# A hybrid encoder block on one core: a fourth place for raw weights, gelu stores on ACT's queue, and two evacuations with higher priority

## The chip, the cores and the metric

The kernel runs on one core of a Trainium2 chip. A core has TensorE (PE, with PEld its weight loads), VectorE (DVE), ScalarE (ACT), GpSimd (POOL) and SyncE (SP), an on-chip memory of 128 partitions, and a smaller accumulator memory in banks of 128x512 f32, into which PE writes. The metric is the device time of one execution in microseconds (us), the median of several runs.

## The reference

One layer for 512 positions of width 1024, everything in f32:

```python
h = _rms(x, norm_mix_g); z = h @ w_in
u_ssm, c_q, c_kv, k_rope = z[:, :512], z[:, 512:1280], z[:, 1280:1536], z[:, 1536:]
# S5 mixer: 32 groups of 16 channels, 64 complex states each, over positions
bu = einsum('gph,bsgh->bsgp', b_bar, u)
states = associative_scan(combine, (a_bar, bu))       # s <- a_bar * s + bu
y = gelu(einsum('ghp,bsgp->bsgh', c, states).real + d_skip * u)
y_ssm = y * sigmoid(y @ w_glu + b_glu)
# latent attention: 8 heads, rotary part of 32, block-causal mask in chunks of 64
q = _rms(c_q, q_norm_g) @ w_q_up;  kv = _rms(c_kv, kv_norm_g) @ w_kv_up
y_mla = softmax(mask(q k^T / sqrt(96))) v
x = x + concat(_rms(y_ssm), _rms(y_mla)) @ w_out
# cross-attention of 4 heads into 256 memory tokens
x = x + xattn(_rms(x), _rms(mem), w_q, w_k, w_v) @ w_o
# experts: best of 4 groups, then the best 2 of its 8 gated experts (hidden 256)
x = x + sum_e gate_e * (silu(h w_gate_e) * (h w_up_e)) @ w_down_e
out = _rms(x, norm_final_g)
```

## The kernel before

The whole program is one stream of instructions that a scheduler sorts for each engine when the program is built; the code gives it a priority, by the place in the program and by `tc.high_priority(n)`, which `hp_(HPW)` uses with n = 150 to put an instruction that many places ahead. Within an engine the order is then fixed: an instruction whose data is not there holds everything behind it. Each engine that issues DMAs has its own queue of such instructions, mixed with its other work; nearly all loads and stores of this kernel are issued on SP.

Weights come through a list. `next_w` takes the next weight, asks for the loads up to `LOOK` ahead (`load_w`, L167, tile `raw`, up to 512 KB), and splits the raw f32 weight into a high part `hi` (ACT, L204) and a rest `lo` (DVE, L214), of which three each are kept. A `raw` place is free when its `lo` is made. A product is three matmuls (L266 hi*hi, L267 hi*lo, L268 lo*hi).

The stages, in the order of the program: the norm of x; the S5 input `pz` (four column blocks; each is evacuated to `zq` by DVE with the row scale, L752, and stored to `zd`); the key and value latent `pkv`; the query latent `pcq` in six blocks of 24 matmuls, evacuated in `cq` (ACT and DVE) and squared into `sq_q` (ACT, L870 and L873), which DVE adds up to `sqa` for the query norm; the norm of the memory tokens (`mem`, `mT`, transposes `pT_norm_mem_g`) with `q_norm` in its middle (column sum `pc_q`, then the rotary tables `crq` and `srq` scaled by it); the query up-projection `pq` in two halves of four position blocks (pq00 to pq03, pq10 to pq13), three weights each; the memory values `pxv`; the latent's keys and values `pv`, `pkn`; attention; the glu, output, cross-attention; and from about 460 us the experts. The accumulators of `pcq`, `pq` and `pxv` share four banks, so pq03 begins where the last `pcq` block has been read.

Between these stages the S5 mixer runs in pieces for four chunk groups q = 0 to 3, each put beside a step of the main stream (`S5_PLAN`): `s5kt` (matmuls, evacuated to `s5k`, stored to `kd` and loaded back as a Toeplitz tile `s_T` by eight loads, L677), `s5vT` (transposes, evacuated to `s5VT`), `s5u` (loaded from `zd`), `s5e` (input matmuls, L696), then on DVE `s5a`, `s5b`, `s5ee`, a scan `s5s` and `s5x` (L707 to L722), `s5y` (output matmuls from `s_T`, `s5u`, `s5G`, `s5x`, L730 and L731), and gelu on ACT into `s5yz` (L735), which eight DMAs of 32 KB store to `gd` (L739), read again only for the glu.

Of the kernel before, what the change touches and what calls it, by code (L numbers as in the profile page):

```python
# [10 lines left out]
F32 = mybir.dt.float32  # L11
# [4 lines left out]
AF = mybir.ActivationFunctionType  # L16
OP = mybir.AluOpType
# [4 lines left out]
NT = 4  # L22
# [77 lines left out]
HPW = 150  # L100
# [4 lines left out]
def build(tc, I, out, dbg=None, stop=None):  # L105
    nc = tc.nc
# [16 lines left out]
    C = es.enter_context(tc.tile_pool(name="const", bufs=1))  # L123
# [1 line left out]
    U = es.enter_context(tc.tile_pool(name="u", bufs=4))  # L125
    B = es.enter_context(tc.tile_pool(name="b", bufs=4, space=PS))
    wes = es.enter_context(ExitStack())
    LOOK = 3
    M = wes.enter_context(tc.tile_pool(name="misc", bufs=2))
    W = wes.enter_context(tc.tile_pool(name="w", bufs=2))  # L130
    raw_es = wes.enter_context(ExitStack())
    WR = raw_es.enter_context(tc.tile_pool(name="raw", bufs=LOOK))
    ses = es.enter_context(ExitStack())
# [6 lines left out]
    def bank(name):  # L140
        return B.tile([128, 512], F32, name=name, tag="mm")

    def bankt(name):
        return B.tile([128, 512], F32, name=name, tag="tr", bufs=2)
# [44 lines left out]
    def next_w(name):  # L189
        i = nxt[0]  # L190
        nxt[0] += 1
        while nxt[1] < min(len(wlist), i + LOOK):
            load_w(nxt[1])
# [45 lines left out]
    for i in range(8):  # L239
# [4 lines left out]
        n, k = divmod(i, 4)  # L244
# [48 lines left out]
    load_w(0, 1)  # L293
    for i in range(1, LOOK):
        load_w(i)
    nxt[1] = LOOK

# [7 lines left out]
    ps = bankt("ps_gx")  # L305
# [3 lines left out]
    def hp_(n):  # L309
        return tc.high_priority(n) if n else nullcontext()  # L310

    def gain(name, k):
        return G[:, gcol[name] + k:gcol[name] + k + 1]
# [57 lines left out]
    def hv(k, c0=0, c1=S):  # L371
        t = hT[k // 2]
        return t[:, k % 2, 0, c0:c1], t[:, k % 2, 1, c0:c1]
# [12 lines left out]
    rx, rx2 = x_st[:, 1], x_st[:, 2]  # L386
    w0 = next_w("ssm")
    rx, rx2 = x_st[:, 1], x_st[:, 2]
# [13 lines left out]
    for t in range(NT):  # L402
        sq = M.tile([128, 2, 512], F32, name=f"xsq{t}", tag="krT", bufs=1)
# [4 lines left out]
    r = 0  # L408
# [4 lines left out]
    ps = bankt("ps_g")  # L413
# [7 lines left out]
    RX = M.tile([128, S], F32, name="RX", tag="krT", bufs=1)  # L421
# [303 lines left out]
    def s5_e(q, b):  # L725
        uu, x2 = b["uu"], b["x2"]
        ps = BS.tile([128, 512], F32, name=f"s5y{q}", tag="s")
        for g in range(8):
            o = ps[:, 64 * g:64 * g + 64]
            nc.tensor.matmul(o, b["T"][:, g], uu[:, g], start=True, stop=False)  # L730
            nc.tensor.matmul(o, b["G"][:, g, 0:8].rearrange("p k h -> p (k h)"), x2[:, g // 2, g % 2],  # L731
                             start=False, stop=True)

        z = M.tile([128, 512], F32, name=f"s5yz{q}", tag="sq")
        nc.scalar.activation(z, ps, AF.Gelu_apprx_tanh)  # L735
        gv = gd[128 * q:128 * q + 128].rearrange("(g h) (j c) -> h j g c", h=16, j=8)
        zz = z.rearrange("p (g c) -> p g c", g=8)
        for j in range(8):
            nc.sync.dma_start(gv[:, 7 - j], zz[16 * j:16 * j + 16])  # L739

    p5 = s5_params()

# [1 line left out]
    for m in range(4):  # L744
        w = next_w("ssm") if m else w0
        ps = bank(f"pz{m}")
        for k in range(8):
            mm3(ps, (w[0][:, k], w[1][:, k]), hv(k), k == 0, k == 7)
        if m == 0 and CX:
            rx_row()  # L750
        z = M.tile([128, 8, 64], F32, name="zq", tag="zq")
        nc.vector.tensor_tensor(z, ps.rearrange("p (c j) -> p j c", j=8), RX.rearrange("p (c j) -> p j c", j=8), OP.mult)  # L752
        nc.sync.dma_start(zd[128 * m:128 * m + 128], z.rearrange("p j c -> p (j c)"))
    sb = [{} for _ in range(4)]

# [22 lines left out]
    nc.vector.tensor_tensor(ang, rpf[:, :, None].to_broadcast([128, NT, 16]),  # L778
                            ivf[:, None, :].to_broadcast([128, NT, 16]), OP.mult)
    sincos(sin, cos, ang, [128, NT, 16], M, "rope")  # L780
    crx, srx = C.tile([128, NT, 16], F32, name="crx"), C.tile([128, NT, 16], F32, name="srx")
    rxb = rx[:, :, None].to_broadcast([128, NT, 16])
    nc.vector.tensor_tensor(crx, cos, rxb, OP.mult)
    nc.vector.tensor_tensor(srx, sin, rxb, OP.mult)
# [78 lines left out]
    for m in range(6):  # L863
        w = next_w("cq")
        ps = bank(f"pcq{m}")
        for k in range(8):
            mm3(ps, (w[0][:, k], w[1][:, k]), hv(k), k == 0, k == 7)
        split(cq[m // 2][:, m % 2, 0], cq[m // 2][:, m % 2, 1], ps, gain("mla_q_norm_g", m))
        if m == 0:
            nc.scalar.activation(sqa, ps, AF.Square)  # L870
        else:
            sq = M.tile([128, S], F32, name=f"sq_q{m}", tag="sq")
            nc.scalar.activation(sq, ps, AF.Square)  # L873
            nc.vector.tensor_tensor(sqa, sqa, sq, OP.add)
        step()
    rq = C.tile([128, NT], F32, name="rq")
    crq, srq = C.tile([128, NT, 16], F32, name="crq"), C.tile([128, NT, 16], F32, name="srq")

    def q_norm():
        colsum_rstd(rq, sqa, 768, "q", True)  # L880
# [79 lines left out]
    for i in range(8):  # L960
        n, c = divmod(i, 4)
# [80 lines left out]
    for hp in range(4):  # L1042
# [16 lines left out]
        else:  # L1059
            sq = M.tile([128, S], F32, name=f"sq_m{hp}", tag="sq")  # L1060
# [20 lines left out]
    for m in range(4):  # L1081
        w = next_w("glu")
        ps = bank(f"pgl{m}")
# [14 lines left out]
        else:  # L1098
            sq = M.tile([128, S], F32, name=f"sq_s{m}", tag="sq")
# [38 lines left out]
    for n in range(2):  # L1138
# [5 lines left out]
        for t in range(NT):  # L1144
            sq = M.tile([128, S], F32, name=f"xsq2{n}{t}", tag="sq")
            square_sum(st2[:, n, t:t + 1], X[t][:, n * 512:n * 512 + 512], sq)
        for k in range(4 * n, 4 * n + 4):
            ps = bankt(f"ph2{k}")
# [421 lines left out]
    for q in OQ:  # L1570
# [5 lines left out]
        else:  # L1576
            g, c = int(q[0]), int(q[1])
# [3 lines left out]
    for c in range(2):  # L1581
        ps = bankt(f"pXt0{c}")
# [70 lines left out]
    ps = bankt("ptab0")  # L1653
# [3 lines left out]
    if T1:  # L1657
        ohb1 = places_of(1)
        ps = bankt("ptab1a")
# [29 lines left out]
    ps = bankt("ptab0w")  # L1689
# [293 lines left out]
```

## Time and profile before

| | |
|---|---|
| median of 3 runs | 716.57 us (715.13 to 717.44) |
| the profiled execution | 717.67 us |
| its span in the trace | 715.9 us |
| PE busy | 666.9 us (93%) |
| DVE busy | 406.1 us (57%) |
| ACT busy | 251.8 us (35%) |
| POOL busy | 113.7 us (16%) |
| DMA moved | 165.83 MB, mean 232 GB/s |
| mean granted TensorE clock | 0.984 |

A row of a timeline gives the start, the duration, the engine, the line of the code, the operation, the output and the inputs with their shapes, and in brackets how long the engine had stood idle and for whom. "SPq" is SP's queue of DMA issues. The profiled execution is 1.1 us over the median, and the span is 1.8 us shorter than that execution's time.

### The profile page before, as it was taken

What the parts mean: (1) busy time and instruction counts of PE and PEld (TensorE: products, weight loads), DVE (VectorE), ACT (ScalarE), POOL (GpSimd) and SP (SyncE); (2) the same over time, 40 slices, a digit from 0 to 9 for tenths busy, and PEclk for the clock granted to TensorE, in tenths of its full rate; (3) what the DMA queues carried; (4) which work ended last, traced back from release to release, by engine and by line L of the source; (5) the groups of instructions that cost most, each with busy time, mean ns of one, the idle gap of its engine ahead of it and who ended that gap; (6) DMA issues with size and microseconds to landing.
All of it is one profiled execution on the core that took longest, in us unless ns stands there. A gap on an engine that the chain in (4) does not pass through costs nothing.

```text
span 715.9 us, 10163 instructions
## 1 busy us (share of the span) xinstructions
PE 666.9 (93%) x3644; PEld 469.7 (66%) x3644; DVE 406.1 (57%) x952; ACT 251.8 (35%) x518; POOL 113.7 (16%) x165
## 2 busy tenths in 40 slices
PE   5989999788999999999999999989999999999793
PEld 4788878676778888888887788734344454454342
DVE  4899988747577887565366642653443512221137
ACT  5734364325666767244344522221000000000023
POOL 6300022002400000102000001212242233233100
PEclk9999999989999999999999999999999999999988
DMA  7763233335452434323328797799999999999993
GB/s 217 199 197 99 66 79 95 79 124 125 112 191 67 147 120 118 95 83 89 91 87 314 274 334 276 240 395 410 405 412 406 411 412 404 410 411 409 381 356 128
DMA packets 102012, 165.83 MB, mean 232 GB/s; under 512 B 32762, under 2 KB 64606, under 8 KB 98120
## 3 DMA queue, kind: packets, MB, share of 16 engines
q1 hardware_dynamic: 95512, 157.58, 62.0%
q0 software_dynamic: 6432, 7.58, 3.1%
q8 instruction: 30, 0.49, 0.3%
q14 instruction: 22, 0.18, 0.1%
q10 hardware_dynamic: 16, 0.00, 0.0%
HBM read 154.59 MB, written 25.69 MB: 252 GB/s over the span
## 4 chain that ended last, share of the span: by engine, by line
PE 59%; DMA 28%; DVE 5%; ACT 4%; issue 1%; SPq 1%; POOL 1%; ACTq 0%; DVEq 0%
DMA gu<-moe_w_up 18%; DMA dn<-moe_w_down 6%; PE pG L1789 3%; PE po L1039 2%; PE pxq L268 2%; PE pxq L267 2%; PE pxq L266 2%; PE pxo L266 2%; DMA raw<-w_in 2%; PE pxo L267 2%; PE pD L1846 1%; PE pxo L268 1%; PE pcq L266 1%; PE pPT L1028 1%; PE pcq L267 1%
## 5 line engine op out<-in xcount | busy, mean ns | idle before, releaser
L1789 PE MATMUL pG<-gu,XT 128*64 128x512 f32 x512 | 120.3, 607 | 6.6 <-DMA gu<-moe_w_up 3.0
L214 DVE TENSOR_TENSOR lo<-raw,hi 128x1024 fp32r<-128x1024 f32 (+3 forms) x64 | 75.5, 1183 | 62.0 <-ACT hi L204 61.5
L204 ACT ACTIVATE hi<-raw 128x1024 fp32r<-128x1024 f32 (+3 forms) x64 | 63.9, 1002 | 107.9 <-issue 26.0
L1789 PEld LDWEIGHTS pG<-gu,XT 128*64 128x64 f32 x512 | 54.5, 139 | 58.7 <-issue 52.0
L1812 DVE SCALAR_TENSOR_TENSOR a<-pG,RS,sl 128x256 f32<-128x256 f32 x16 | 10.7, 671 | 113.2 <-ACT sl L1806 106.8
L1846 PE MATMUL pD<-dn,aT 128*64 128x512 f32 x256 | 71.1, 600 | 0.5 <-ACT aT L1832 0.5
L1806 ACT ACTIVATE sl<-pG,RS 128x256 f32<-128x256 f32 x16 | 7.6, 473 | 123.5 <-PE pG L1789 123.5
L1846 PEld LDWEIGHTS pD<-dn,aT 128*64 128x64 f32 x256 | 22.4, 137 | 35.7 <-issue 34.4
L1855 DVE SCALAR_TENSOR_TENSOR YY<-pD,GT,YY 128x512 f32<-128x512 f32 x26 | 19.5, 750 | 25.2 <-PE pD L1846 25.1
L1808 POOL TENSOR_SCALAR YY<-XG,F 128x1024 f32<-128x1024 f32 x13 | 14.5, 1116 | 114.8 <-issue 50.7
L1832 ACT ACTIVATE aT<-pA 128x256 f32<-128x256 f32 x16 | 6.1, 384 | 68.0 <-PE pA L1830 36.4
L1772 PEld LDWEIGHTS pX<-ident,XG 128*128 128x128 f32 x120 | 14.6, 194 | 16.9 <-issue 12.9
L267 PE MATMUL pxq<-gT,hi 128*128 128x512 f32 x64 | 25.6, 400 | 0.0
L266 PE MATMUL pxq<-gT,hi 128*128 128x512 f32 x64 | 25.5, 399 | 0.0
L268 PE MATMUL pxq<-gT,lo 128*128 128x512 f32 x64 | 25.4, 396 | 0.0
L1417 DVE TENSOR_TENSOR XT<-pX,gmo 128x512 f32<-128x512 f32 x30 | 19.3, 683 | 7.4 <-PE pX L1772 7.4
L1772 PE MATMUL pX<-ident,XG 128*128 128x128 f32 x120 | 17.6, 288 | 3.8 <-DMA XG<-hd,IX 3.8
L1388 POOL TENSOR_TENSOR st_moe<-st_moe 128x1 f32<-128x1 f32 x4 | 0.8, 190 | 118.6 <-issue 104.4
L266 PE MATMUL pcq<-hT,hi 128*128 128x512 f32 x48 | 19.2, 401 | 0.0
L268 PE MATMUL pcq<-hT,lo 128*128 128x512 f32 x48 | 19.1, 398 | 0.0
L267 PE MATMUL pxv<-lo,mT 128*128 128x512 f32 x32 | 13.9, 435 | 5.5 <-DVE lo L214 5.5
L267 PE MATMUL pcq<-hT,hi 128*128 128x512 f32 x48 | 18.9, 395 | 0.0
(614 smaller groups left out, 1670.6 us busy)
## 6 DMA issues: line engine op xcount, KB each, us to landing
gu<-moe_w_gate SPq DMA_DIRECT2D x64, 512.0 KB
gu<-moe_w_up SPq DMA_DIRECT2D x64, 512.0 KB
dn<-moe_w_down SPq DMA_DIRECT2D x30, 1024.0 KB
raw<-w_in SPq DMA_DIRECT2D x9, 512.0 KB
raw<-xattn_w_v SPq DMA_DIRECT2D x8, 512.0 KB
raw<-xattn_w_k SPq DMA_DIRECT2D x8, 512.0 KB
raw<-w_out SPq DMA_DIRECT2D x8, 512.0 KB
raw<-xattn_w_q SPq DMA_DIRECT2D x8, 512.0 KB
```

Source lines behind the costliest of these rows:

```text
L204: anchor["act"] = nc.scalar.activation(hi, r, AF.Copy)
L214: anchor["dve"] = nc.vector.tensor_tensor(lo, r, hi.bitcast(F32), OP.subtract)
L266: i = nc.tensor.matmul(o, lh, rh, start=start, stop=False)
L267: nc.tensor.matmul(o, lh, rl, start=False, stop=False)
L268: anchor["pe"] = nc.tensor.matmul(o, ll, rh, start=False, stop=stop)
L1039: nc.tensor.matmul(po[64 * s:64 * s + 64, b * 128:b * 128 + 128], V[:, k, 64 * h:64 * h + 64], PTs[s][:, k * 128:k * 128 + 128], start=k = ...
L1417: return v.tensor_tensor(xt, ps.rearrange("p (k t) -> p k t", k=4), gmo[:, 4 * c:4 * c + 4, None].to_broadcast([128, 4, 128]), OP.mult)
L1772: i = nc.tensor.transpose(ps[:, k * 128:k * 128 + 128], xg[:, 4 * c + k], ident)
L1789: i = nc.tensor.matmul(pg[64 * s:64 * s + 64], xt[c][:, kk, 64 * s:64 * s + 64], ew[2 * n + s, c][:, :, kk], start=k == 0, stop=k == 7)
L1808: nc.gpsimd.tensor_scalar(result(n), XG[n % 2], F1[:, n:n + 1], 1.0, OP.mult, OP.mult)
L1846: i = nc.tensor.matmul(pd[64 * s:64 * s + 64], at_[:, f, 64 * s:64 * s + 64], ew[2 * n + s, 2][:, f, c * 512:c * 512 + 512], start=f == 0, ...
L1855: yield v.scalar_tensor_tensor(o, pd, GT[:, n:n + 1], o, OP.mult, OP.add)
```

## The change

Four edits. `LOOK` goes from 3 to 4, so the raw weights have four places and are asked for one weight earlier; the memory for it comes from the rotary tables of the key (`crx`, `srx`) and of the query (`crq`, `srq`), which now share a place each. The eight gelu stores of each chunk group are issued by ACT and no longer by SP. The evacuation `zq` and the squares of the query blocks 1 to 5 are issued under the priority of 150.

```diff
@@ -125,7 +125,7 @@
     U = es.enter_context(tc.tile_pool(name="u", bufs=4))
     B = es.enter_context(tc.tile_pool(name="b", bufs=4, space=PS))
     wes = es.enter_context(ExitStack())
-    LOOK = 3
+    LOOK = 4
     M = wes.enter_context(tc.tile_pool(name="misc", bufs=2))
     W = wes.enter_context(tc.tile_pool(name="w", bufs=2))
     raw_es = wes.enter_context(ExitStack())
@@ -736,7 +736,7 @@
         gv = gd[128 * q:128 * q + 128].rearrange("(g h) (j c) -> h j g c", h=16, j=8)
         zz = z.rearrange("p (g c) -> p g c", g=8)
         for j in range(8):
-            nc.sync.dma_start(gv[:, 7 - j], zz[16 * j:16 * j + 16])
+            nc.scalar.dma_start(gv[:, 7 - j], zz[16 * j:16 * j + 16])
 
     p5 = s5_params()
 
@@ -749,7 +749,9 @@
         if m == 0 and CX:
             rx_row()
         z = M.tile([128, 8, 64], F32, name="zq", tag="zq")
-        nc.vector.tensor_tensor(z, ps.rearrange("p (c j) -> p j c", j=8), RX.rearrange("p (c j) -> p j c", j=8), OP.mult)
+        with hp_(HPW):
+            nc.vector.tensor_tensor(z, ps.rearrange("p (c j) -> p j c", j=8), RX.rearrange("p (c j) -> p j c", j=8),
+                                    OP.mult)
         nc.sync.dma_start(zd[128 * m:128 * m + 128], z.rearrange("p j c -> p (j c)"))
     sb = [{} for _ in range(4)]
 
@@ -778,7 +780,7 @@
     nc.vector.tensor_tensor(ang, rpf[:, :, None].to_broadcast([128, NT, 16]),
                             ivf[:, None, :].to_broadcast([128, NT, 16]), OP.mult)
     sincos(sin, cos, ang, [128, NT, 16], M, "rope")
-    crx, srx = C.tile([128, NT, 16], F32, name="crx"), C.tile([128, NT, 16], F32, name="srx")
+    crx, srx = (C.tile([128, NT, 16], F32, name=n + "rx", tag=n + "r") for n in "cs")
     rxb = rx[:, :, None].to_broadcast([128, NT, 16])
     nc.vector.tensor_tensor(crx, cos, rxb, OP.mult)
     nc.vector.tensor_tensor(srx, sin, rxb, OP.mult)
@@ -870,11 +872,12 @@
             nc.scalar.activation(sqa, ps, AF.Square)
         else:
             sq = M.tile([128, S], F32, name=f"sq_q{m}", tag="sq")
-            nc.scalar.activation(sq, ps, AF.Square)
+            with hp_(HPW):
+                nc.scalar.activation(sq, ps, AF.Square)
             nc.vector.tensor_tensor(sqa, sqa, sq, OP.add)
         step()
     rq = C.tile([128, NT], F32, name="rq")
-    crq, srq = C.tile([128, NT, 16], F32, name="crq"), C.tile([128, NT, 16], F32, name="srq")
+    crq, srq = (C.tile([128, NT, 16], F32, name=n + "rq", tag=n + "r") for n in "cs")
 
     def q_norm():
         colsum_rstd(rq, sqa, 768, "q", True)
```

The lines behind move by two (from L753) and by three (from L874).

What it moves, at three places. First SP's queue around the store of chunk group 1. Before (raw is a weight's load, gd the gelu store, kd, s5u and s_T belong to the next chunk group):

```order
L167 DMA raw_1548<-mla_w_q_up 128x2x384
L167 DMA raw_1613<-xattn_w_v 128x2x512
L167 DMA raw_1643<-xattn_w_v 128x2x512
L739 DMA gd<-s5yz_1349 16x8x64 x8
L673 DMA kd_220<-s5k_1398 4x32x256
L686 DMA s5u_1611<-zd 128x8x64
L167 DMA raw_1758<-xattn_w_v 128x2x512
L677 DMA s_T_379<-kd_220 16x1024
L677 DMA s_T_379<-kd_220 16x8x112
```

After:

```order
L677 DMA s_T_382<-kd_221 16x8x16
L167 DMA raw_1426<-mla_w_q_up 128x2x384
L167 DMA raw_1550<-xattn_w_v 128x2x512
L167 DMA raw_1615<-xattn_w_v 128x2x512
L686 DMA s5u_1613<-zd 128x8x64
L673 DMA kd_222<-s5k_1400 4x32x256
L167 DMA raw_1645<-xattn_w_v 128x2x512
L677 DMA s_T_381<-kd_222 16x1024
L677 DMA s_T_381<-kd_222 16x8x112
```

The eight stores are gone from this queue, and kd and s5u of the next chunk group stand one value weight earlier: raw_1645 (raw_1643 before) now follows kd, and the next weight, raw_1758 before, comes behind the eight s_T.

Second, ACT's queue around the gelu of chunk group 0. Before:

```order
L672 ACTIVATE s5k_1057<-s5kt_1048 128x2x112
L329 ACTIVATE mT_1219,st_norm_mem_g<-mem 128x1024
L684 ACTIVATE s5VT<-s5vT_1069 128x512
L684 ACTIVATE s5VT<-s5vT_1075 128x512
L329 ACTIVATE mT_1219,st_norm_mem_g<-mem 128x1024
L338 ACTIVATE mem<-mem,st_norm_mem_g 128x1024 x2
L276 ACTIVATE cq_722<-pcq_1102,G 128x512
L204 ACTIVATE hi_1361<-raw_1145 128x768
L276 ACTIVATE cq_722<-pcq_1151,G 128x512
L204 ACTIVATE hi_1426<-raw_1302 128x768
L873 ACTIVATE sq_q_1129<-pcq_1102 128x512
L873 ACTIVATE sq_q_1178<-pcq_1151 128x512
```

After:

```order
L735 ACTIVATE s5yz_1040<-s5y_1023 128x512
L672 ACTIVATE s5k_1059<-s5kt_1050 128x2x112
L739 DMA gd<-s5yz_1040 16x8x64 x4
L876 ACTIVATE sq_q_1131<-pcq_1104 128x512
L739 DMA gd<-s5yz_1040 16x8x64 x4
L684 ACTIVATE s5VT<-s5vT_1071 128x512
L684 ACTIVATE s5VT<-s5vT_1077 128x512
L329 ACTIVATE mT_1221,st_norm_mem_g<-mem 128x1024 x2
L276 ACTIVATE cq_724<-pcq_1153,G 128x512
L338 ACTIVATE mem<-mem,st_norm_mem_g 128x1024 x2
L876 ACTIVATE sq_q_1180<-pcq_1153 128x512
```

The stores stand in ACT's order as two groups of four around a sq_q; one cq, two hi and that sq_q now stand ahead of them or of the table load, and the last sq_q (1180, before 1178) comes behind the two mem scalings. The same rows with the semaphores that each waits for:

```order
L739 DMA gd<-s5yz_1040 16x8x64 [waits DMAHW7_49,Activation_49]
L739 DMA gd<-s5yz_1040 16x8x64 [waits DMAHW2_49]
L739 DMA gd<-s5yz_1040 16x8x64 [waits DMAHW4_49]
L739 DMA gd<-s5yz_1040 16x8x64 [waits DMAHW6_49]
L876 ACTIVATE sq_q_1131<-pcq_1104 128x512 [waits DVE_49]
```

DMAHW0 to DMAHW7 are eight counters of landed transfers that the DMAs of SP and ACT use in turn; a store has a wait for an earlier transfer on its counter.

Third, PE's queue. Before, at the start of the output matmuls s5y of chunk group 1, in the second half of the query up-projection:

```order
L266 MATMUL pq_1546<-hi_1615,cq_721 128x384
L267 MATMUL pq_1546<-lo_1616,cq_721 128x384
L268 MATMUL pq_1546<-hi_1615,cq_721 128x384
L266 MATMUL pq_1546<-hi_1615,cq_721 128x384
L267 MATMUL pq_1546<-lo_1616,cq_721 128x384
L268 MATMUL pq_1546<-hi_1615,cq_721 128x384
L730 MATMUL s5y_1332<-s5u_1081,s_T_380 128x64
L731 MATMUL s5y_1332<-s5x_1210,s5G_936 128x64
```

After, at the start of the same s5y, in the first half, ahead of which stands s5e of the same group:

```order
L696 MATMUL s5e_1183<-s5u_1083,s5VT 64x64 x16
L266 MATMUL pq_1303<-hi_1306,cq_722 128x384
L267 MATMUL pq_1303<-lo_1307,cq_722 128x384
L268 MATMUL pq_1303<-hi_1306,cq_722 128x384
L353 MATMUL pc_q<-ones_103,sq_q 128x1 x4
L345 MATMUL pT_norm_mem_g_1250<-ident,mem 128x128 x2
L266 MATMUL pq_1303<-hi_1306,cq_722 128x384
L267 MATMUL pq_1303<-lo_1307,cq_722 128x384
L345 MATMUL pT_norm_mem_g_1255<-ident,mem 128x128 x2
L268 MATMUL pq_1303<-hi_1306,cq_722 128x384
L730 MATMUL s5y_1334<-s5u_1083,s_T_382 128x64
L731 MATMUL s5y_1334<-s5x_1212,s5G_938 128x64
```

These output matmuls have moved from behind most of the second half's matmuls to right behind the first transposes of the memory norm, and s5e, their input, stands behind 36 matmuls of pq instead of ahead of them.

## The prediction

> **What bounds the kernel now.** I read the busy time by stage first: it tells which engine sets the pace where. The columns are the stage, its length, the busy time of PE, PE's weight loads, DVE, ACT and POOL, the granted clock, the DMA share and GB/s.
>
> ```profile
> 40.00:60.00 20.00, 17.69 (x111) 16.86 (x111) 19.11 (x61) 6.78 (x13) 0.11 (x1) 0.91 0.61 171
> 80.00:100.00 20.00, 20.00 (x148) 16.76 (x147) 19.03 (x22) 9.51 (x15) 4.63 (x5) 1.00 0.29 67
> 100.00:120.00 20.00, 17.01 (x102) 15.60 (x101) 17.82 (x37) 11.77 (x23) 3.88 (x15) 1.00 0.36 104
> 140.00:160.00 20.00, 14.72 (x84) 12.22 (x85) 11.03 (x26) 3.77 (x4) 0.12 (x1) 0.83 0.38 127
> 220.00:460.00 240.00, 239.66 (x1330) 196.56 (x1329) 145.22 (x306) 110.27 (x222) 11.82 (x31) 1.00 0.50 167
> 460.00:680.00 220.00, 206.97 (x998) 97.67 (x998) 74.56 (x223) 20.28 (x52) 62.66 (x62) 1.00 1.02 402
> ```
>
> From 220 to 460 PE is busy for 239.66 of 240 us; from 460 to 680 the DMA engines are full (share 1.02, 402 GB/s) with expert weights. Those loads go into places that PE's earlier work frees, so I count what PE gains before 220 one for one at the end. PE idles 2.3 us in 40 to 60, 3.0 in 100 to 120 and 5.3 in 140 to 160, and the edits lie in this front part. The waits from 40 to 220 say for what (who waited for whom, total us, times, longest):
>
> ```profile
> PE pxv L267 <- DVE lo L214: 5.5, 2, 5.2
> PE pkv L266 <- DVE zq L752: 2.3, 1, 2.3
> PE pxv L266 <- DVE rp1q L793: 1.3, 1, 1.3
> PE pkrT L836 <- DVE ckT L277: 1.3, 1, 1.3
> PE pv L267 <- DVE lo L214: 1.2, 1, 1.2
> PE pq L266 <- ACT sq_q L873: 1.2, 1, 1.2
> PE pT_norm_mem_g L345 <- DVE mT L277: 0.9, 1, 0.9
> ...
> PE pq L266 <- DVE rp1q L793: 0.7, 1, 0.7
> ...
> SPq L739 <- ACT s5yz L735: 29.4, 3, 13.4
> ```
>
> The last line is SP's queue over 0 to 220: with a gelu store at its head it stood 29.4 us, 13.4 at once. SP and ACT show what was behind it:
>
> ```profile
> 130.69 4.34 SPq L739 DMA_DIRECT2D gd<-s5yz  x8
> ...
> 136.31 0.53 SPq L167 DMA_DIRECT2D raw<-xattn_w_v  x1
> 139.49 5.00 SPq L677 DMA_DIRECT2D s_T<-kd  x8
> ...
> 142.08 1.06 ACT L204 ACTIVATE hi<-raw 128x1024 fp32r<-128x1024 f32 x1 [3.08 <-DMA raw<-xattn_w_v]
> ```
>
> PE pays for it in the value projection:
>
> ```profile
> 138.33 0.40 PE L266 MATMUL pxv<-hi,mT 128*128 128x512 f32 x1
> 140.07 0.47 PE L266 MATMUL pxv<-hi,mT 128*128 128x512 f32 x1 [1.34 <-DVE rp1q L793]
> 145.75 0.80 PE L267 MATMUL pxv<-lo,mT 128*128 128x512 f32 x1 [5.21 <-DVE lo L214]
> ...
> 155.28 0.39 PE L268 MATMUL pxv<-hi,mT 128*128 128x512 f32 x1
> 155.51 0.33 PE L730 MATMUL s5y<-s5u,s_T 128*128 128x64 f32 x2
> ```
>
> **Gelu stores on ACT's queue and the fourth raw place: what goes.** The weight that hi waited for was asked for at 136.31, behind the stores. In the new order it stands behind the eight s_T loads of the next chunk group (5.00 us on SP), but that group's S5 work stands earlier too, its first matmuls soon after the moved s5y; I estimate s_T issued by 129 and the weight asked for at 129 to 131. It took 5.8 us to reach hi at 142.08 in the profile; by 137 it is there, and PE comes to it at 142 or later (the waits below). From 138.33 to 155.51 PE runs 36 matmuls that, back to back, start 0.233 us apart (the last, 155.28 to 155.51): 8.4 us, so it would be done at 146.7. That is 8.8 us earlier; 6.55 of it are the two waits, the rest the slow clock that follows (below). Bounds: 8.8 if both waits go; 5.2 if only the long one goes. I take −8.8, because in the new order the rotary evacuations that made the 1.34 us wait also stand well ahead.
>
> **What comes back at gelu 0.** In the new order ACT works through: table load, s5yz, s5k, four stores, one sq_q, four stores, two s5VT, two mT, cq, two mem, and only then the last sq_q. The last sq_q frees the bank on which the fourth block of query matmuls (pq03) starts. The prices, from the timelines of ACT, SP, PE and DVE:
>
> ```profile
> 92.17 0.60 ACT L735 ACTIVATE s5yz<-s5y 128x512 f32<-128x512 f32 x1
> 92.79 3.67 SPq L739 DMA_DIRECT2D gd<-s5yz  x8
> 95.16 1.09 ACT L684 ACTIVATE s5VT<-s5vT 128x512 f32<-128x512 f32 x2 [0.45 <-PE s5vT L683]
> 96.13 1.06 ACT L329 ACTIVATE mT<-mem 128x1024 fp32r<-128x1024 f32 x1
> 99.65 1.16 ACT L338 ACTIVATE mem<-mem,st_norm_mem_g 128x1024 f32<-128x1024 f32 x1 [1.23 <-POOL st_norm_mem_g L318]
> 100.71 0.67 ACT L276 ACTIVATE cq<-pcq,G 128x512 fp32r<-128x512 f32 x1
> 105.66 0.60 ACT L873 ACTIVATE sq_q<-pcq 128x512 f32<-128x512 f32 x1 [1.75 <-DVE cq L277]
> 98.51 1.15 PE L696 MATMUL s5e<-s5u,s5VT 128*64 128x64 f32 x32
> 99.88 0.34 PE L267 MATMUL pq<-lo,cq 128*128 128x384 f32 x1
> 100.05 0.34 PE L268 MATMUL pq<-hi,cq 128*128 128x384 f32 x1
> 103.96 0.44 PE L266 MATMUL pq<-hi,cq 128*128 128x384 f32 x1 [1.18 <-ACT sq_q L873]
> 105.48 0.68 DVE L707 TENSOR_TENSOR s5a<-s5e,s5tb 128x512 f32<-128x512 f32 x1
> 112.64 0.42 DVE L722 TENSOR_TENSOR s5x<-s5a,s5b 64x252 f32<-64x252 f32 x1
> ```
>
> The squares put ahead also leave a cq and a sq_q in front of the gelu's table load (0.67 and 0.60, and the cq must wait for its matmuls); I estimate the gelu 2 us later, at 94.2, and s5k done near 95. Behind it: eight stores 3.67 (SP's price; another queue may differ), sq_q 0.60, two s5VT 1.09, two mT 2.1, cq 0.67, two mem 2.3, the POOL wait 1.23, sq_q 0.60: 12.3 us, so the last sq_q ends near 107.3. But each store also waits, in the new order, for an earlier transfer of SP to be counted as landed. No row shows such a wait on ACT; I bound it by 0 and by 4 us (nearest: a group of four stores, half of 3.67, twice over) and take 2: 109.3. PE, meanwhile, has 36 query matmuls (0.174 us apart, 6.3 us) and s5e (1.1) from 98.5: it stands at pq03 from 105.9. A wait of 3.4 where it had 1.18.
>
> Right behind, the new order has the output matmuls of S5 chunk group 1 (s5y), which stood some 60 matmuls later. They need s5x. From s5a to the last s5x took 105.48 to 113.06, 7.6 us; with s5e ending at 105.9, s5x is not there before 113.5. PE's unstalled work from 98.5 to that point is 10.2 us (108.7), so it has idled 4.8 by then against 1.4 before: +3.4, however early the last sq_q is. Later in this stretch PE lost 0.9 (mT) and 0.7 (rp1q): if these vanish, +1.8 in all; if the transposes behind the query norm, which now follow that s5y at once, wait as long as zq's 2.3, +5.7. I take +4.0, nearer the lower end since both are single waits.
>
> **The clock.** The 2.3 us wait of PE for zq, up to 46.1, was followed by a slow clock, the 1.18 us one up to 103.96 was not (columns as in the first view):
>
> ```profile
> 46.00:48.00 2.00, 1.91 (x12) 1.94 (x13) 2.00 (x2) 0.21 (x1) 0.00 (x0) 0.80 0.84 224
> 48.00:50.00 2.00, 2.00 (x10) 2.00 (x10) 2.00 (x3) 0.84 (x1) 0.00 (x0) 0.50 1.05 300
> 104.00:106.00 2.00, 2.00 (x12) 2.00 (x13) 2.00 (x4) 0.34 (x1) 0.00 (x0) 1.00 0.27 29
> ```
>
> After the zq wait the granted clock is 0.80 for 2 us and 0.50 for 2 us: 0.4 + 1.0 = 1.4 us lost. The stretch after the long wait costs 8.8 − 6.55 = 2.2 us at most. A wait of 3.4 at pq03 is longer than zq's 2.3, so I add one slow stretch, +1.4 (0 to 2.9 for none or two).
>
> [...]
>
> **Other terms.** zq ahead: its 2.31 us wait (40 to 60) shrinks, since zq no longer stands behind other work of DVE. But DVE is busy 19.1 of 20 us there and 19.0 in 80 to 100, and PE next meets it at s5y of group 0, which needs DVE's whole chain up to s5x; what PE gains at 46 it would wait there. Without that cover it would be −3.7, the wait and its slow stretch; a further delay +0.5; I take 0. The fourth raw load at the start stands ahead of the gains: one 512 KB transfer at the 171 to 300 GB/s of the rows from 40 to 60 is 1.7 to 3.1 us, of which PE's other matmuls cover most: +0.5 (0 to 3.1). Gelu 2: eight stores (3.67) on ACT ahead of s5VT and hi: +0.9 (0 to 2.5; the nearest rows are the waits for ckT and lo, 1.3 and 1.2, which would come twice). Gelu 3: seven stores ahead of a weight's hi: +0.4 (−1.0, if pv's wait for lo goes, to +3.7, all the stores' price). Expert weights queue on SP behind the last raw loads, which go one deeper; DMA is half busy (0.50) before 460, so some may start earlier: −1.3 if the full stage gets by with one 512 KB load less at 402 GB/s, 0 if places decide; −0.6. The rotary tables' shared place: 0, since the first pair has had its last reader, the key's rotation, before the query norm writes the second. A store that lands later hurts nobody in these stages: gd is read back only behind the attention.
>
> Sum: −8.8 + 4.0 + 1.4 + 0 + 0.5 + 0.9 + 0.4 − 0.6 = −2.2. The profiled execution is 717.67 (715.9 of span), 1.1 above the median 716.57; it becomes 715.5, the median 714.4.
>
> **Rivals.** (1) Paid back in full: gelu 0 at 5.0 in place of 4.0 and gelu 3 at the middle of its bounds, 1.4 in place of 0.4: −0.2, 716.4. For it: each is a real queue. Against: hand-followed waits often overlap.
> (2) Slower. ACT's queue becomes what SP's was: a store waiting for a transfer holds the evacuations, and PE waits for banks. At gelu 0 the 4.0 becomes 5.7, with a second slow stretch 1.4 becomes 2.9, at gelu 2 2.5 and at gelu 3 3.7: −8.8 + 5.7 + 2.9 + 0.5 + 2.5 + 3.7 − 0.6 = +5.9, 722.5; its middle is 720. It decides from 4.4 us of stores' waits on PE's path, that is a last sq_q after about 112 or a gelu 3 store that waits for the load issued last. For it: SP's 13.4 us show how long a queue can stand; against: ACT has 8 to 16 us of each 20 free in the stages shown from 80 to 160.
> [...]
> (3) The stall goes and little comes back: stores do not wait, s5y's cover holds, small waits go: −8.8 + 1.8 − 1.0 − 1.3 = −9.3, 707.3.
> (4) The change doesn't do what it says: raw loads are still late, since DVE's lo frees their places; −5.2 in place of −8.8: 718.0. It sits inside (1) and (2).
>
> **Chances.** My forecast (712 to 715.5) 0.36, (1) 0.25, (2) 0.27, (3) 0.12. A measurement here tells about 0.3% (2.15 us) from no change. Faster by more: (3) and most of the forecast, 0.46; within: (1) and the rest, 0.26; slower: 0.28. The range leaves out the far ends of (2) and (3): 707 to 721.
>
> **What would show it.** Right: no wait of PE for lo in the value projection, and SP's wait for s5yz gone; PE waiting 2 to 4 us for sq_q near 106 and for s5x before an early s5y; s5yz's stores as ACT's queue work with idle behind them. Wrong: a last sq_q before 106 and s5y without a wait (then rival 3), or ACT standing over 4 us at a store (rival 2), or PE still waiting for lo of a value weight (rival 4).

## The result: 1.3% slower

The changed kernel takes 726.77 us (median of 4 runs, 725.51 to 729.85) against 717.01 for the kernel before in the same runs: ratio 1.0129, interval 1.0103 to 1.0155. The forecast was 714.4, range 707 to 721. The profiled execution has a span of 724.8 us where before had 715.9.

The changed kernel by stage, with the columns of the first view of the prediction:

```profile
40.00:60.00 20.00, 18.79 (x134) 16.94 (x132) 19.93 (x69) 9.27 (x18) 0.11 (x1) 1.00 0.68 191
...
100.00:120.00 20.00, 15.32 (x98) 14.32 (x98) 13.34 (x26) 10.15 (x17) 4.73 (x19) 0.65 0.32 82
140.00:160.00 20.00, 20.00 (x126) 17.48 (x126) 10.92 (x30) 6.88 (x13) 0.12 (x1) 1.00 0.50 148
180.00:200.00 20.00, 14.25 (x66) 10.65 (x65) 9.69 (x12) 9.86 (x15) 5.58 (x5) 0.83 0.62 197
```

PE is now busy all the time from 140 to 160, the worst of these stretches before. The losses sit in 100 to 120, where the granted clock is 0.65, and in 180 to 200. PE's waits from 40 to 220 (total us, times, longest):

```profile
PE pq L266 <- ACT sq_q L876: 4.7, 2, 4.1
PE pxv L266 <- ACT hi L204: 4.6, 1, 4.6
...
PE pkv L266 <- DVE zq L753: 0.3, 1, 0.3
```

The wait for lo in the value projection is gone and the one for zq is down from 2.3 to 0.3; the one for the last squares has grown from 1.2 to 4.1, and one for a weight's hi is new.

Idle time alone does not explain the loss. I cut both traces where the last matmul of the same work starts, and in each stage summed PE's idle time, and its busy time times (1 − granted clock), that is the work that a slow clock stretched. Length in us, with idle and slow in brackets:

| stage ends with the last matmul of | before | changed | change |
|---|---|---|---|
| (first 40 us) | 40.0 (7.9, 0.0) | 40.0 (7.3, 0.0) | |
| pcq | 58.2 (2.3, 1.7) | 55.3 (1.2, 0.0) | −2.9 |
| pq | 40.0 (3.1, 0.0) | 48.5 (5.3, 7.2) | +8.5 |
| pv | 45.2 (9.3, 1.9) | 39.6 (1.6, 0.0) | −5.6 |
| psc (scores) | 78.8 (1.9, 0.0) | 86.5 (8.4, 3.5) | +7.7 |
| pgl (glu) | 20.0 (0.1, 0.0) | 21.2 (0.4, 0.0) | +1.2 |
| pxo (cross-attention's output) | 175.1 (0.2, 0.0) | 175.2 (0.2, 0.0) | +0.1 |

The sum is +9.0 at pxo, and the span is longer by 8.9: what is lost in front arrives at the end. Over these stages idle time is about equal (24.8 and 24.4), and slow clock grows from 3.6 to 10.7. Together that is 6.7 of the 9.0; for the other 2.3 PE was busy at full clock, and what it did in them was not traced. (Stages do not hold exactly the same S5 pieces, so a single stage's change is good to a few us; the sum is not touched by that. All of it is one execution of each kernel: the profiled one of the changed kernel has a mean granted clock of 0.973, its other three 0.976 to 0.981.)

The place in the stage pq. First PE, in windows of 2 us (busy time, granted clock, DMA share, GB/s), then the ACT rows that set it:

```profile
104.00:106.00 2.00, 0.20 (x8) 1.00 0.69 191
106.00:108.00 2.00, 0.00 (x0) 0.52 0.00 0
108.00:110.00 2.00, 1.33 (x3) 0.50 0.00 0
...
112.00:114.00 2.00, 2.00 (x10) 0.50 0.00 0
...
120.00:122.00 2.00, 2.00 (x11) 0.50 0.18 66
122.00:124.00 2.00, 2.00 (x20) 0.71 0.61 137
```

```profile
92.88 2.34 ACTq L739 DMA_DIRECT2D gd<-s5yz  x4
98.04 0.60 ACT L876 ACTIVATE sq_q<-pcq 128x512 f32<-128x512 f32 x1 [4.94 <-DVE cq L277]
98.04 3.09 ACTq L739 DMA_DIRECT2D gd<-s5yz  x4
101.18 1.09 ACT L684 ACTIVATE s5VT<-s5vT 128x512 f32<-128x512 f32 x2 [2.55 <-DMA gd<-s5yz]
...
107.66 0.57 ACT L876 ACTIVATE sq_q<-pcq 128x512 f32<-128x512 f32 x1
```

The last squares end at 108.2, PE goes on at 108.3 after 4.1 us, and the clock, down since 106.1, comes back only near 123.2, after 17.1 us at half (0.52 in the window from 106 and 0.71 in the one from 122 give the two ends). From 112 to 122 PE is busy without a gap. The stores are not all that holds ACT here: between the two groups of four it stands from 95.2 to 98.0 until DVE has made cq.

And the place in the stage psc. ACT's timeline:

```profile
180.97 0.60 ACT L735 ACTIVATE s5yz<-s5y 128x512 f32<-128x512 f32 x1 [2.92 <-PE s5y L731]
...
182.03 1.06 ACT L204 ACTIVATE hi<-raw 128x1024 fp32r<-128x1024 f32 x1 [0.46 <-ACT s5yz L735]
182.05 7.85 ACTq L739 DMA_DIRECT2D gd<-s5yz  x7
189.95 2.00 ACT L204 ACTIVATE hi<-raw 128x1024 fp32r<-128x1024 f32 x2 [6.86 <-DMA raw<-xattn_w_k]
```

SP's timeline, and the stores of the line L739 alone, from 184 to 185 us and from 189 to 190 (min, median and longest issue in ns, first and last start):

```profile
169.34 0.61 SPq L167 DMA_DIRECT2D raw<-xattn_w_v  x1
170.04 1.33 SPq L167 DMA_DIRECT2D raw<-xattn_w_k  x2
...
185.26 0.37 SPq L167 DMA_DIRECT2D raw<-xattn_w_k  x1
```

```profile
L739 ACTq DMA_DIRECT2D gd<-s5yz x1: 449/449/449, 184.7 to 184.7; - x1
...
L739 ACTq DMA_DIRECT2D gd<-s5yz x1: 309/309/309, 189.6 to 189.6; - x1
```

The value weight whose hi PE waits for was asked for at 169.34. Its hi, the first of the two in the last ACT row, starts at 189.95, because seven stores stand ahead of it on ACT. Six of them are out by 185.2; the last stands until 189.6. In ACT's order that store waits for the counter DMAHW7, whose transfer before it is the key weight that SP had asked for only at 185.26: in the trace that transfer has landed in full at 189.58, the store goes out at 189.60, and the profile names the landing of a key weight as what ended ACT's wait of 6.9 us. So a weight in hand waits, through a store, for a later weight.

### The profile page after: what moved, and what is told of

Its sections match the earlier page's. It is cut to its first block, busy times and chain, and to the rows that moved or that the text cites. A ratio compares the mean times of both kernels' runs of the same rounds, so it can differ in the third digit from the quotient of the medians.

```text
span 724.8 us, 10160 instructions
## 1 busy us (share of the span) xinstructions
PE 675.7 (93%) x3644; PEld 474.0 (65%) x3644; DVE 406.8 (56%) x952; ACT 251.5 (35%) x518; POOL 108.8 (15%) x165
## 4 chain that ended last, share of the span: by engine, by line
PE 49%; DMA 32%; DVE 10%; ACT 3%; SPq 2%; issue 2%; ACTq 0%; DVEq 0%
DMA gu<-moe_w_up 21%; DMA dn<-moe_w_down 6%; PE po L1042 2%; DVE lo L214 2%; PE pxq L266 2%; PE pxq L267 2%; PE pxq L268 2%; PE pxo L266 2%; DMA raw<-w_in 2%; PE pxo L267 2%; PE pxo L268 1%; PE pPT L1031 1%; DMA xb<-xd 1%; PE pG L1792 1%; PE pcq L266 1%
## 5 line engine op out<-in xcount | busy, mean ns | idle before, releaser
L1815 DVE SCALAR_TENSOR_TENSOR a<-pG,RS,sl 128x256 f32<-128x256 f32 x16 | 10.7, 671 | 112.3 <-ACT sl L1809 105.9
L266 PE MATMUL pq<-hi,cq 128*128 128x384 f32 x48 | 17.4, 365 | 4.7 <-ACT sq_q L876 4.7
L266 PE MATMUL pcq<-hT,hi 128*128 128x512 f32 x48 | 19.3, 403 | 1.0 <-DVE s_ph-1_768 L601 1.0
L266 PE MATMUL pxk<-mT,hi 128*128 128x256 f32 x64 | 19.6, 306 | 0.1
L268 PE MATMUL pxk<-mT,lo 128*128 128x256 f32 x64 | 19.2, 300 | 0.0
```

Of the source, the lines that this page charges most:

```text
L266: i = nc.tensor.matmul(o, lh, rh, start=start, stop=False)
L268: anchor["pe"] = nc.tensor.matmul(o, ll, rh, start=False, stop=stop)
```

## The experiments

Ratios are to the kernel before in shared runs; its median was 717.0 to 718.2 us in them, so ratios, not single medians, are to be compared.

**Undo one edit: the stores back on SP.**

```diff
-            nc.scalar.dma_start(gv[:, 7 - j], zz[16 * j:16 * j + 16])
+            nc.sync.dma_start(gv[:, 7 - j], zz[16 * j:16 * j + 16])
```

> The changed kernel with the gelu stores issued by SP again; the fourth raw place and the two priorities stay. Theory C (the stores on ACT cause two waits of PE, 4.1 and 4.6 us, and what they cost is mostly the slow clock behind them): 713 to 718 us, no slow stretch of 16 us after 104, the wait of the last squares back to 1 to 2 us. Theory R (the deeper raw loads and the priorities, which reorder DVE and SP, are what costs): 724 to 728.

Measured: 738.6 us, 1.0288 (1.0267 to 1.031). Neither theory's number; the direction is theory R's. Against SP's queue, the stores on ACT save 12 us in the changed kernel.

**One edit alone: the stores on ACT.**

> The kernel before with one edit, the gelu stores issued by ACT. Theory C: 721 to 728 us, with a wait of PE for the last squares of 3 us or more and more than 10 us of clock at 0.50 in the whole trace (before: 5.1 us lost to the slow clock). Theory R: 715 to 719.

Measured: 723.34 us, 1.0069 (1.0045 to 1.0092). The expected waits are there:

```profile
PE pq L266 <- ACT sq_q L873: 5.3, 1, 5.3
PE s5e L696 <- ACT s5VT L684: 4.8, 1, 4.8
PE pxv L266 <- ACT hi L204: 3.9, 1, 3.9
```

The time is in theory C's range. All three waits are for ACT work that stands behind stores: in ACT's timeline eight stores take 7.3 us up to 100.8, ahead of what leads to the last squares, 7.8 us up to 159.9, ahead of s5VT, and 7.8 us up to 187.9, ahead of hi. The edit costs 4.9 us in all with three raw places; how much of it each wait makes was not separated. The changed kernel's other edits add some 4 us net.

The clock does something else here than in the changed kernel. The wait for the squares is longer (5.3 us, PE goes on at 107.93), yet the clock is down only from 104.5 to 111.4 (columns as in the first view):

```profile
108.00:110.00 2.00, 2.00 (x6) 2.00 (x7) 1.96 (x3) 2.00 (x4) 0.10 (x1) 0.50 0.00 0
110.00:112.00 2.00, 2.00 (x9) 2.00 (x9) 2.00 (x4) 0.82 (x2) 0.11 (x1) 0.66 0.59 163
```

Behind this wait stand matmuls of pq with 384 columns, and no s5y.

**The first chunk group's stores on SP, the rest on ACT.**

```diff
-            nc.scalar.dma_start(gv[:, 7 - j], zz[16 * j:16 * j + 16])
+            (nc.sync if q == 0 else nc.scalar).dma_start(gv[:, 7 - j], zz[16 * j:16 * j + 16])
```

> The changed kernel with the first chunk group's eight stores on SP, the other 24 on ACT. Theory C: the wait at pq03 and the 16.5 us of half clock behind it go, worth 2.9 + 8.3 us: 714 to 718. A theory of order alone (the early output matmuls of chunk group 1 are what costs by waiting for their input, not the clock): they move back to the second half of the query projection here too, but only the 2.9 us of idle go: 723 to 725.

Measured: 736.59 us, 1.0257 (1.0221 to 1.0293). A miss for both. The half clock over 16 us is gone, yet the stage to pv grew to 64.2 us (39.6 in the changed kernel): s5y of chunk group 1 starts at 127.55, as with all stores on SP (127.93), and no longer at 113.73. That this order is what lost more is argued from the stage, not shown.

**Filler in the wait.** Twenty matmuls whose result nobody reads, right after s5e of chunk group 1.

```diff
+        if q == 1:
+            wb = BS.tile([128, 512], F32, name="warm", tag="s")
+            for _ in range(20):
+                nc.tensor.matmul(wb, cq[0][:, 0, 0, 0:128], cq[0][:, 0, 0, :], start=True, stop=True)
         pv = ps.rearrange("p (a k c) -> p a k c", a=2, k=4)
```

> The changed kernel with 20 extra matmuls of 128x512 (about 0.233 us each, 4.7 us) after s5e of chunk group 1, where PE then stands 4.1 us; their result is read by nobody. Theory C: the granted clock stays at 1.00 from 104 to 122, which returns 8 us less about 0.6 for the fillers that outlast the wait: 718 to 721. If idle and not the clock is the cost: 726 to 728.

Measured: 725.2 us, 1.0097 (1.0064 to 1.013), outside theory C's 718 to 721. The filler's row, the windows of 20 us, and PE's longest wait show that the clock part of theory C held there and the total did not:

```profile
104.51 4.83 PE L702 MATMUL warm<-cq 128*128 128x512 f32 x20
```

```profile
100.00:120.00 20.00, 19.68 (x161) 1.00 0.37 93
120.00:140.00 20.00, 18.97 (x133) 1.00 0.36 98
140.00:160.00 20.00, 14.42 (x90) 0.83 0.30 98
```

```profile
PE pxv L267 <- DVE lo L214: 6.6, 1, 6.6
```

The clock is 1.00 from 100 to 140, the stage pq takes 42.4 us in place of 48.5, and the value projection begins 5.8 us earlier. There PE then stands 6.6 us for lo, the kind of wait that the change had removed, and the clock drops in it. In this kernel's order three lo stand behind S5's chain on DVE (144.30, right after the last s5x). The stage up to pv takes 58.8 us (11.7 idle, 8.4 slow) in place of 39.6, the next one 74.3 in place of 86.5. The filler moved the order of every engine, so this run shows what it does to the clock in the wait, not what that clock is worth in the total; its interval overlaps the changed kernel's.

**One edit alone: the fourth raw place** (with the shared rotary places, which give it its memory).

```diff
-    LOOK = 3
+    LOOK = 4
```

> The kernel before with one edit, the fourth raw place (and the shared rotary places). Theory D (the fourth place is what costs, since with the stores back on SP the changed kernel took 738.6 us): 733 to 740 us. Rival P (the priorities of zq and the squares cost): 715 to 719.

Measured: 736.24 us, 1.0248 (1.0229 to 1.0267). Theory D. The shared rotary places leave every engine's order as it was when made alone, so the place itself is left, with the loads that it lets SP ask for earlier. The stage psc takes 92.7 us (6.8 idle, 6.7 slow) in place of 78.8.

**One edit alone: the two priorities.**

> The kernel before with one edit, the priorities of zq and of the squares. Theory D: 714 to 719 us, the 2.3 us wait for zq gone and little else. Rival P: 728 to 740.

Measured: 716.05 us, 0.9977 (0.9962 to 0.9993), theory D. The wait for zq is gone, and 1.4 of the some 2 us are already won when pcq ends.

**The stores on POOL, all other edits kept.**

```diff
-            nc.scalar.dma_start(gv[:, 7 - j], zz[16 * j:16 * j + 16])
+            (nc.gpsimd).dma_start(gv[:, 7 - j], zz[16 * j:16 * j + 16])
```

> The changed kernel with the gelu stores issued by POOL, so that they stand in neither SP's nor ACT's order. If the stores on ACT are what costs (4.1 and 4.6 us of waits and the slow clock behind): 710 to 718 us. If the fourth raw place costs whatever queue the stores are on (theory D): 725 to 740.

Measured: 714.04 us, 0.9927 (0.9903 to 0.9951): theory D's "whatever queue" is wrong. With the stores on neither SP nor ACT the fourth place costs some 3.5 us (against the run with three places below).

**The stores on POOL in the kernel before.**

> The kernel before with the gelu stores issued by POOL and nothing else. If SP's queue behind the stores made the 6.6 us of waits in the value projection: 706 to 713 us, without the 5.2 us wait. If the weight comes late for another reason (the place in the raw pool, the s_T loads ahead of it): 715 to 719 with the wait still there.

Measured: 711.52 us, 0.9906 (0.9887 to 0.9924). The 5.2 us wait is gone; SP's timeline, and the stage 140 to 160:

```profile
127.21 0.36 SPq L167 DMA_DIRECT2D raw<-xattn_w_v  x1
130.43 4.99 SPq L677 DMA_DIRECT2D s_T<-kd  x8
```

```profile
140.00:160.00 20.00, 20.00 (x146) 16.49 (x146) 11.69 (x23) 9.76 (x19) 4.16 (x8) 1.00 0.51 135
```

The weight that was asked for at 136.31 before is asked for at 127.21, and PE does not stand at all from 140 to 160. S5's chain on DVE is earlier too: it starts at 127.50 (137.98 before), and the first value weight's lo at 132.81.

**The stores on POOL and the two priorities, three raw places.**

> The kernel before with the stores on POOL and the two priorities, three raw places. If the edits add up (711.5 - 2.2): 708 to 711. If the priorities only gain where PE has an SP wait to hide behind: 711 to 713.

Measured: 710.27 us, 0.9879 (0.9848 to 0.991), the lowest median of all. That is what the two gains added would give, but its interval overlaps that of the stores on POOL alone (0.9887 to 0.9924), so that the priorities gain here too is not shown.

**Four places, asked for three ahead.**

```diff
-    WR = raw_es.enter_context(tc.tile_pool(name="raw", bufs=LOOK))
+    WR = raw_es.enter_context(tc.tile_pool(name="raw", bufs=4))
```

> The kernel before with four raw places but loads asked for three ahead as before (the rotary tables share their places). If the 18 us of the fourth place come from loads that are asked for earlier and stand on SP ahead of S5's loads: 715 to 720. If they come from the place itself (other order of the S5 pieces on PE and DVE, shared tables): 730 to 738.

`LOOK` stays at 3. Measured: 734.11 us, 1.0222 (1.0187 to 1.0257). The cost is there without the earlier requests on SP, so it comes with the place. That it acts through the order that the scheduler makes of it is argued: PE's, DVE's, ACT's and SP's orders all differ from those before, and the stage psc takes the same 92.7 us as with the place and the earlier requests.

**Only the first, or only the last chunk group's stores on ACT, the rest on POOL.**

```diff
-            nc.scalar.dma_start(gv[:, 7 - j], zz[16 * j:16 * j + 16])
+            (nc.scalar if q == 0 else nc.gpsimd).dma_start(gv[:, 7 - j], zz[16 * j:16 * j + 16])   # other run: q == 3
```

> The changed kernel with the first chunk group's stores on ACT and the other 24 on POOL. The theory that the first group's stores hold the last squares, and the clock then stays at half over the early S5 output matmuls: 3 us of wait and 6 to 8 us of slow clock over the 714.0 of the kernel with all stores on POOL, 720 to 726. If that wait is hidden elsewhere: 713 to 716.

> The changed kernel with the last chunk group's stores on ACT and the other 24 on POOL. The theory that these stores hold a weight's hi for a transfer of SP, as the changed kernel's 4.6 us wait shows: 4 to 8 us over 714.0, 718 to 722. If that wait came from the lateness of what is ahead: 713 to 716.

Measured: 719.52 us, 1.0028 (1.0011 to 1.0046), and 714.11 us, 0.9951 (0.993 to 0.9973). The first is just under the 720 to 726 expected, the second the other reading's 713 to 716. Against all stores on POOL (714.04) the first group costs 5.5 us by the medians, 7.3 by the ratios. The last squares end at 108.4 in place of 103.5, and the stage pq is 48.7 us (5.3 idle, 7.5 slow) against 41.7 (3.6, 1.5), nearly the numbers of the changed kernel. The last group costs nothing that can be told in the total (the intervals overlap). Its stores do hold hi for as long as in the changed kernel,

```profile
176.43 8.28 ACTq L739 DMA_DIRECT2D gd<-s5yz  x8
184.83 1.06 ACT L204 ACTIVATE hi<-raw 128x1024 fp32r<-128x1024 f32 x1 [8.44 <-DMA gd<-s5yz]
```

and the stage psc takes 3.0 us more than with POOL, but the rest of that kernel's order gained as much elsewhere.

**DVE's order or SP's queue.** In the kernel before, hi of the first value weight starts at 130.56, but its lo starts only at 144.48, behind S5's chain on DVE. Here lo of five value weights gets a higher priority.

```diff
-                anchor["dve"] = nc.vector.tensor_tensor(lo, r, hi.bitcast(F32), OP.subtract)
+                with tc.high_priority(100) if 19 <= i <= 23 else nullcontext():
+                    anchor["dve"] = nc.vector.tensor_tensor(lo, r, hi.bitcast(F32), OP.subtract)
```

> The kernel before with one edit: lo of the first five value weights is issued under a higher priority, so that on DVE two of them stand ahead of S5's chain instead of behind it. Stores stay on SP, three raw places. Theory O (the 5.2 us wait in the value projection is DVE's order: lo stood behind the S5 chain though its hi was ready 13 us earlier): 708 to 713 us, the wait gone. Theory Q (the prediction's: SP's queue behind the stores made the weight late): 715 to 719, the wait still there or moved to hi.

Measured: 716.91 us, 0.9986 (0.9967 to 1.0006): no difference that can be told, which is theory Q's number. Two lo now come early, and the wait shrinks from 5.2 to 3.1 us and moves to a later weight (the timelines of DVE, SP and PE):

```profile
138.86 1.22 DVE L215 TENSOR_TENSOR lo<-raw,hi 128x1024 fp32r<-128x1024 f32 x1
...
141.13 1.22 DVE L215 TENSOR_TENSOR lo<-raw,hi 128x1024 fp32r<-128x1024 f32 x1
...
151.01 2.59 DVE L215 TENSOR_TENSOR lo<-raw,hi 128x1024 fp32r<-128x1024 f32 x2
```

```profile
139.19 0.53 SPq L167 DMA_DIRECT2D raw<-xattn_w_v  x1
```

```profile
152.29 0.79 PE L268 MATMUL pxv<-lo,mT 128*128 128x512 f32 x1 [3.10 <-DVE lo L215]
```

The next weight is still asked for behind the stores (139.19). Two causes stood one behind the other, and neither theory alone was right; the stores on POOL took away both.

**The fourth place with those lo ahead** (the same line with 300 for 100).

> The kernel before with the fourth raw place (736 us alone) and the value weights' lo ahead on DVE. If the fourth place costs by the late lo (6.6 us of wait and the slow clock behind): 722 to 728. If by what comes after the value projection (S5's last group beside the first scores, 93 us in place of 79): 730 to 736.

Measured: 720.11 us, 1.0034 (1.0008 to 1.0059), better than either theory expected: 15 to 16 of the fourth place's 18 us are gone. The longest wait for lo in the value projection is 1.9 us in place of 6.6, and the stage psc is 82.3 us (3.9, 1.7) in place of 92.7. A priority on five instructions of DVE cannot bring that by their own 6 us alone; it also changed where the scheduler put the pieces behind them. How much of the 16 is the lo and how much the rest stays open.

**Wide matmuls in the slow clock.** Sixteen matmuls ahead of the early s5y, into its bank, which s5y then overwrites.

```diff
+        for _ in range(16 if q == 1 else 0):
+            nc.tensor.matmul(ps, cq[0][:, 0, 0, 0:128], cq[0][:, 0, 0, :], start=True, stop=True)
```

> The changed kernel with 16 extra matmuls of 128x512 around the transposes ahead of the early S5 output matmuls, where the clock is at 0.50 for 16 us; their result is overwritten. If the clock returns after some 4 us of dense wide matmuls and the 16 us came from the narrow ones there (64 columns): clock at 1.00 from about 118 in place of 122.6, S5's output matmuls at full speed, time within 2 us of 726.8. If the length of the slow stretch is fixed by the wait before it: clock at 0.50 to 122 and 3 to 4 us more, 730.

Measured: 729.11 us, 1.015 (1.0113 to 1.0186). The wait is nearly the same (3.8 us, PE goes on at 108.62), and the windows are:

```profile
108.00:110.00 2.00, 1.33 (x3) 0.65 0.00 0
...
114.00:116.00 2.00, 1.96 (x7) 0.64 0.44 84
116.00:118.00 2.00, 1.31 (x8) 1.00 0.46 178
...
122.00:124.00 2.00, 2.00 (x20) 1.00 0.00 0
```

The clock is down for 6.8 us in place of 17.1. It is back near 115.4, while the first four wide matmuls run (from 114.35) and sooner than either theory had it, and s5y runs at full speed. The slow work falls from 7.2 to about 3 us in that stage; the fillers themselves take time, and the total, 2.3 us over the changed kernel's, is no better. So behind nearly the same wait (3.8 and 4.1 us) the slow stretch was 6.8 or 17.1 us long: the wait alone did not fix its length, and by their edit the two kernels differ in what PE does behind it.

## Why the prediction was wrong

Two terms failed, and both price what the stores on ACT cost: the slow clock behind gelu 0's wait, put at +1.4 and +7.2 in its stage, and gelu 3, put at +0.4 and +7.7 in its stage. The gain that the sum began with did come. By its own terms, against the stage table:

- **The main term, −8.8: right in size, half right in its reason.** In the stage up to pv, idle and slow fall by 7.7 + 1.9 = 9.6 us (the stage is only 5.6 shorter, as more of S5 lies in it). The stores on SP did make the weight late (asked for at 127.21 without them), but the row that the prediction quoted named DVE's lo, and of the first weight hi had been ready 13 us before its lo. I read "PE waits for lo" as "the weight came late" and did not ask when hi and raw were there. In the changed kernel the load was asked for at 134.03 (129 to 131 was forecast). That is the third value weight, as the load at 136.31 before was, and it stands ahead of the eight s_T (from 135.64): the fourth place asks for each weight one earlier, and the one behind s_T in the changed order is the fourth value weight, so pairing it with the load at 136.31 was a misreading. What saved PE there was the lo's place on DVE (138.56, ahead of most of S5's chain), and that PE came 5.6 us later (143.97 against 138.33).

```profile
143.97 0.39 PE L266 MATMUL pxv<-hi,mT 128*128 128x512 f32 x1
```

```profile
134.03 0.38 SPq L167 DMA_DIRECT2D raw<-xattn_w_v  x1
```

- **Gelu 0, +4.0: right in mechanism, and its time in part luck.** The last squares were put at 109.3 and ended at 108.2; the wait at pq03 was put at 3.4 and was 4.1. But the gelu came at 92.25 and not 94.2, and the 2.8 us that ACT stood for DVE's cq between the stores, which the sum did not have, made up for it. S5's early output matmuls followed as said, but did not wait for s5x. Idle time in the stage grew by 2.2, little over half of the term.
- **The clock, +1.4 (bound 2.9): the step that failed.** The term was priced from the stretches after two other waits, both followed by wide matmuls (288 and 512 columns). For the zq wait it also left out the window from 50 to 52, with which the loss there is 1.7 and not 1.4:

```profile
50.00:52.00 2.00, 2.00 (x15) 2.00 (x14) 2.00 (x6) 0.00 (x0) 0.00 (x0) 0.85 0.59 133
```

In the changed kernel the wait was followed, but for a few matmuls of pq, by the column sums, the transposes and s5y with 64 columns, and the clock stayed at half for 17.1 us: +7.2 in this stage. e11 gives 7.5 for the first group alone, e4 takes it away, e15 cuts it short with wide matmuls, and in e2 a longer wait with wide matmuls behind it costs 1.7. Over all stages the slow clock grew by 7.1.
- **Gelu 3, +0.4 (bound 3.7): the other step that failed, in size.** The mechanism was named in the second rival: a store that waits for the load issued last, and the trace shows it (the last store, 4.5 us). The idle time of the stage rose by 6.5 and the slow work by 3.5, together 10.0, more than the stage's +7.7, so other work has left it. The bound took SP's price for eight stores, 3.7 us; on ACT they took 7.85 (seven) and, in e12, 8.28 (eight) from the first to the last. That this place costs 7.7 by itself is not shown: e12 with only these stores on ACT lost 3.0 there and nothing that can be told in the total.
- **zq ahead, 0: a gain that was denied.** The stage up to pcq is 2.9 us shorter, and s5y of group 0 starts at 81.23 against 84.18; the priorities alone bring some 2 us (e6). DVE was busy, but what PE gained at zq it did not wait out at s5y of group 0.
- **Gelu 2, +0.9:** nothing of it is seen; the stage up to pv idles 1.6 us in all. **Expert weights, −0.6:** nothing; the 9.0 at pxo are the 8.9 of the span.
- **The fourth place, +0.5 at the start: wrong in kind.** It was costed only as one load more ahead of the gains. Alone it costs 17.8 us (1.0248); as far as e10 and e14 go, through another order of S5's pieces and of lo on DVE. With the stores on POOL most of that cost is absent: 714.0 with it and the priorities, 710.3 without it.

The edits do not add up: +2.5% for the place, +0.7% for the stores on ACT and −0.2% for the priorities would be +3.0%, and the change is +1.3%. The stores and the place each make the scheduler lay the whole stretch from 95 to 200 anew: s5y of chunk group 1, for one, starts at 126.29 before, 128.68 with the place alone, 112.37 with the stores alone on ACT and 113.73 with all edits. What is shown is where the time is lost in the changed kernel and that the stores of the first group on ACT cost 5.5 us (7.3 by the ratios) of the 12.7 (14.5) between all stores on POOL and all on ACT. The rest of these comes only with the other groups' stores; the last group alone does not bring it, the two in the middle were not run alone, and its split stays open.

Rival 2 was the right one: the kernel is slower, and of its two signs the store at gelu 3 that waits for the load issued last was there, while the last squares came before 112. It was given 0.27, and its price of 722.5 still lacked the long slow clock.

## What to carry to other kernels

In the changed kernel a wait of PE cost its own length and then the clock, and the clock's part went with what stood behind the wait: 17.1 us at half with transposes and 64-column matmuls behind a wait of 4.1 us, 6.8 us where 512-column ones were put ahead of s5y behind one of 3.8 us (e15), and 6.8 us with 384-column ones behind one of 5.3 us (e2). Price it from a stretch followed by the same kind of matmuls, and look at what small matmuls stand behind a stall. Stores that waited held what stood behind them on their engine (hi on ACT for 6.9 us), so they are best put where little stands behind them that PE needs: here POOL (−0.9%), not ACT (+0.7%). And a buffer more is not a local change under a scheduler that sorts the whole program: here the fourth place cost 2.5% although no transfer needed it.

## What the runs showed of the hardware

- After a wait of 4.1 us the granted clock stayed at 0.50 for 17.1 us, of which PE was busy without a gap for the last 11, mostly on transposes and 64-column matmuls. In e4 it stayed at 0.50 from 176 to 182 too, with PE busy all the time, from 176.7 on with s5y. With wide matmuls put in the same place (e15) it was low for 6.8 us, and after a wait of 5.3 us with 384-column matmuls behind it (e2) for 6.8.
- In these two traces the lengths come in steps. Worked out from the 2 us windows, the stretches of half clock up to 220 us are 3.4 (47.2 to 50.6) and 6.8 (142.8 to 149.6) before, and 17.1, 6.8 (188.0 to 194.8) and 3.4 (201.7 to 205.1) in the changed kernel: 1, 2 or 5 times 3.41. They do not start with the wait: in the changed kernel the clock fell 1.9 us after PE stood, in e15 3.8 us after it, when the wait was over, and before only when PE was at work again for 1.1 us (zq). That what a wait costs depends also on when it falls would fit this, but no run shows it.
- In e15 PE had been busy for 4.6 us when the clock returned, 1.1 of them on wide matmuls. In the changed kernel PE was busy from 112 to 122 too, and the clock stayed at 0.50.
- A store by itself took its issuing engine 0.43 to 0.53 us in the median; its wait took the rest. All 32 stores by queue (before, changed, and the kernel before with POOL's queue; min, median and longest issue in ns):

```profile
L739 SPq DMA_DIRECT2D gd<-s5yz x32: 325/430/882, 92.8 to 191.2; - x32
```

```profile
L739 ACTq DMA_DIRECT2D gd<-s5yz x32: 309/442/742, 92.9 to 189.6; - x32
```

```profile
L739 POOL DMA_DIRECT2D gd<-s5yz x32: 528/528/628, 93.3 to 181.1; - x32
```

Eight of them are about 3.5 us of issue on SP or ACT and 4.2 on POOL. The 7.85 us that seven took on ACT are 3.4 of issue and one wait of about 4.5 for a transfer.

- In each of the two traces the 380 DMAs that SP and ACT issue count their landings on eight semaphores (100 and 102 to 108; the four stores of gelu 0 that wait for DMAHW7, 2, 4 and 6 count on 108, 103, 105 and 107), in turn: in order of time the next issue is on the next of the eight in 377 of 379 steps before, where one of them is ACT's, and in 346 in the changed kernel, where 33 are. There 26 of the 32 stores wait for the very semaphore that they then count on.
